# A PEER expert sweep walked by pairs of chunks instead of single chunks, with paired weight loads

## The chip, the core and the metric

The kernel is one program on one of the eight cores of a Trainium2 chip. The metric is device time in microseconds (us) of the whole program; lower is better. "PE" is the matrix engine, "DVE" the vector engine, "ACT" the scalar engine, "POOL" the engine that issues the gathers, "SP" the engine that issues the plain loads. All loads and gathers run on the same 16 DMA engines: what SP issues goes through queue q1 in the profile, what POOL issues through q0. Four runs of the kernel before were made: three for the time and one under the profiler.

## The reference

One decoder layer on 512 tokens of width 1024, in float32. First a mixer: eight heads of dilated window attention and eight of stick-breaking attention from one combined projection, an output projection, a residual and a LayerNorm. Then a PEER layer, cut here to what matters:

```python
q = (x @ w_query)                               # 8 heads, 2 halves of 128
scores = einsum(q, sub_keys)                    # 128 scores per half
top-16 per half -> 256 sums -> top-16 -> softmax gates, expert_idx in 0..16383
u = expert_u[expert_idx]                        # 128 experts per token
h = einsum('td,ted->te', x, u)
act = gates * gelu(h)
y = einsum('te,ted->td', act, expert_v[expert_idx])
x = LayerNorm(ALPHA * x + y)
```

The tables expert_u and expert_v have 16384 rows of 1024 floats, 64 MB each.

## The kernel before

The 512 tokens are four blocks of 128. The PEER layer is computed in two ways at once.

**Blocks 0 and 1, by gathers.** For each token and each of its 128 selected experts a row is fetched: one indirect DMA (`gather`, L790) fetches one selected row for each of 128 tokens, 512 KB in rows of 4 KB. There are 512 of them: 128 of U and 128 of V for block 0, then the same for block 1. The generator `gathers` (L826) issues them up to eight ahead of their use. A use (`gather_use`, L803) is one DVE instruction over 128 x 1024: a dot product for U (L808), a multiply-add into an accumulator for V (L819). A gather's buffer comes free with its use.

**Blocks 2 and 3, densely.** All 16384 experts are swept in 128 chunks of 128 experts, for the 256 tokens of both blocks. Chunk c has two parts:

- H(c), `h_part` (L918): eight products of a U chunk with the tokens, then a GELU on ACT (`gelu`, L910). The U chunk is loaded by `load_u` (L905) from a transposed copy of the table, 512 KB in rows of 4 KB, into one of WBUF = 4 buffers.
- Y(c), `y_mm` (L1229): the activation of the chunk, times its gates, times the V chunk, accumulated over all chunks. Most chunks are split into a high and a low part, three products each: `split_v` (L1177) rounds V on ACT (L1186) and subtracts on DVE (`low`, L126), `act_prep` (L1206) multiplies by the gates on DVE (L1210, L1211), rounds on ACT (L1221) and subtracts on DVE (L1227). The chunks that `plain` (L1174) names go through in one float32 product without a split. A split V buffer is free after the split; that of a plain chunk only after its Y.

The gates lie densely in memory: an earlier stage of 64 "gate steps" (one-hot products, `one_hot_b`, `gated`, `one_hot_2`, `g_mm`, `g_out`) writes them to a DRAM scratch `gd`, and the sweep reads them back in groups of eight chunks (`load_g`, L1026, called for chunk c+4 after chunk c; 960 KB in rows of 7.5 KB into one of two buffers `gt`).

**Order of the work.** The program runs in the order in which the Python code records it; each engine has one queue and goes through it strictly in order, so that an instruction that waits holds up all that stand behind it. The H parts of the first LEAD = 40 chunks are recorded early (`run_ahead`, L933), as filler of PE between other work; a burst of them runs in the routing of block 2 and some in each gate step. In the late gate steps, once the routing of blocks 3 and 1 is done, every fourth step also takes one gather (L1158). Then comes the main loop (L1303), for c from 0 to 121: `split_all(c)` prepares V up to chunk c+1 (more towards the end) and activations in pairs of chunks, then come as many gather uses as keep pace with a goal that reaches 512 at c = 116 (L1305; before c = 88 each chunk counts 1, after it 0.75), then H(c+40) while there is one, Y(c), the load of U chunk c+43, a group of gates, and V loads as far as buffers allow (`upto("l", ...)`, two pools of two buffers). H of the last chunk stands at c = 87; from c = 88 on pairs of chunks alternate between plain (88, 89, 92, 93, ... 120, 121) and split. The Y of the last KT = 6 chunks follow the loop (L1326 to L1332), first for block 2 over both halves, then for block 3, each with its LayerNorm (`final`, L1241) and output. The LayerNorms of blocks 0 and 1 are recorded into the loop, block 0 from c = 89 on, block 1 after the last gather.

Of the kernel before, what the change touches and what calls it, by code (L numbers as in the profile page):

```python
# [74 lines left out]
VBUF = 4  # L75
# [19 lines left out]
def build(ctx, nc, tc, a):  # L95
# [16 lines left out]
    wst = open_pool(ctx, "wst", "left", 2)  # L112
# [805 lines left out]
    def h_part(c, k0, k1):  # L918
        if k0 == 0:
            hps[c] = ps_h.tile([P, 512], F32, name="h", bufs=2)  # L920
        for k in range(k0, k1):
            nc.tensor.matmul(hps[c][:, :ND], us[c][:, k], xf[:, k], start=k == 0, stop=k == KD - 1)  # L922
# [10 lines left out]
    def run_ahead(n):  # L933
        out = None
        for _ in range(n):
            nxt_ = next(ahead, None)
            if nxt_ is None:
                break
            c, k = nxt_
            if k == 0:  # L940
                load_u(c + 3)
                if c and c - 1 in hps:
                    out = c - 1
            h_part(c, k, k + 1)
        if out is not None:
            gelu(out, hps.pop(out))
# [67 lines left out]
    r1 = open_pool(ctx, "r1", "right")  # L1014
# [17 lines left out]
    def load_v(c):  # L1032
        if c >= P:
            return
        vs[c] = vq[c // 2 % 2].tile([P, D], F32, name="v", bufs=2)
        nc.sync.dma_start(vs[c], a["peer_v"][c * P:(c + 1) * P])

    with tc.manual_schedule():
# [9 lines left out]
        for i in range(-1, NTASK + 2):  # L1048
# [30 lines left out]
            if i == 2 * NH:  # L1079
                for c in range(3):  # L1080
                    load_u(c)
# [5 lines left out]
        qs.close()  # L1087
        up = open_pool(ctx, "up", "left")
# [61 lines left out]
        for n in range(2):  # L1150
            load_v(n)
# [15 lines left out]
        rqs.close()  # L1167
        sgs.close()
        gtp.append(open_pool(ctx, "gt1", "left"))
        vq.append(open_pool(ctx, "vq1", "left"))  # L1170
        load_v(2)
# [18 lines left out]
        for c, k in ahead:  # L1190
            if k == 0:
                load_u(c + 3)
# [48 lines left out]
        def final(tb):  # L1241
# [7 lines left out]
            else:  # L1249
                y = wst.tile([P, D], F32, name="w", bufs=WBUF)  # L1250
# [20 lines left out]
        nxt = {"v": 1, "a": 2, "l": 3}  # L1271

        def upto(kind, last, use, at=P):
            now = []
            for c in range(nxt[kind], min(last, P - 1) + 1):
                if kind == "l" and plain(c - VBUF) and c - VBUF > at:
                    break
                now.append(c)
            nxt[kind] += len(now)
            for c in now:  # L1280
                use(c)
            return now

        def upto_a(last):
            now = []
            while nxt["a"] <= min(last, P - 1):
                c = nxt["a"]
                n = 2
                nxt["a"] += n
                act_prep(c, n, 1)  # L1290
                now.append((c, n))
            return now

        def split_all(c):
            ext = max(0, c - (P - 11))
            nv = upto("v", min(c + 5, c + 1 + (c > P - LEAD) + ext, nxt["l"] - 1), lambda k: split_v(k, 1))
            na = upto_a(c + 1 + max(0, ext - 1))
            for k in nv:
                split_v(k, 2)
            for k in na:  # L1300
                act_prep(*k, 2)

        for c in range(P - KT):  # L1303
            split_all(c)
# [7 lines left out]
            h_mm(c + LEAD)  # L1312
            for t in range(2):
                y_mm(t, c)
            load_u(c + LEAD + 3)
            load_g(c + 4)
            upto("l", nxt["v"] + 2, load_v, c)
            if c == P - LEAD:
                nc.scalar.preload_act_table_set("natural_log_exp_and_others")
                todo2 = final(0)  # L1320
                ln2 = []
                for n in ("ln2_g", "ln2_b"):
                    ln2.append(wst.tile([P, D], F32, name="w", bufs=WBUF))
                    nc.sync.dma_start(ln2[-1], a[n].to_broadcast([P, D]))
        upto("l", P, load_v)
        for c in range(P - KT, P):  # L1326
            split_all(c)
# [14 lines left out]
def layout(inputs):  # L1342
# [12 lines left out]
        "uT": f["peer_u"].reshape(P, P, KD, P).transpose(0, 3, 2, 1),  # L1355
# [19 lines left out]
```

## Time and profile before

| | us |
|---|---|
| median of three runs | 1468.81 (1466.58 to 1469.32) |
| time of the profiled execution | 1463.64 |
| its span, first to last instruction | 1461.9 |
| work ahead of the main loop's first Y | 0 to 744.8 |
| main loop with H and Y, c = 0 to 87 | 744.8 to 1288.3 |
| main loop with Y alone, to the last gather use | 1288.3 to 1414.6 |
| from there to the end | 1414.6 to 1461.9 |

The span is 1.7 us shorter than the execution's own time, and that execution is 5.2 us faster than the median of the three runs. PE is busy for 1375.1 us (94%), DVE 1176.7 (80%), POOL 672.0 (46%), ACT 479.1 (33%). A busy share is an average over stages with different limits; which one ends last is read stage by stage. A row of the timeline gives start, length, engine, line, operation, output<-inputs and, in brackets, the idle time ahead of it and what ended it.

### The profile page before, as it was taken

Reading aid. Unit: us, or ns where it says so; the run is one execution under the profiler, and the core shown is the slowest. Engines: PE = TensorE matmul, PEld = TensorE weight load, DVE = VectorE, ACT = ScalarE, POOL = GpSimd, SP = SyncE. Lnnn points to the kernel's source line nnn. Section 1 sums busy time; section 2 is a strip of 40 time slices with the busy share of each in tenths; the row PEclk is TensorE's granted clock in tenths of the full one; section 3 lists DMA queues with packets and bytes.
Section 4 is the critical chain, followed back from the end, with each engine's and each line's share of the span. In section 5 each row is a group of like instructions: output and inputs, shape, how many; then the busy total and the mean of one; then the engine's idle time right before and its main releaser. Section 6 shows DMA issues by size and latency. Waiting matters only on the chain.

```text
span 1461.9 us, 19349 instructions
## 1 busy us (share of the span) xinstructions
PE 1375.1 (94%) x6570; PEld 1101.9 (75%) x6570; DVE 1176.7 (80%) x2443; ACT 479.1 (33%) x962; POOL 672.0 (46%) x526
## 2 busy tenths in 40 slices
PE   8997999999989999799999999999999999987887
PEld 4676877766659998688988888888888888854444
DVE  1258998778789999899878877877777878798896
ACT  1322344264422111489932222222222222221121
POOL 0003577668554433100146566655555655656620
PEclk9999999999889999899999999999999999999999
DMA  8787899799889989767899999999999999999982
GB/s 297 252 268 280 299 368 321 276 377 343 303 290 376 329 286 317 240 182 207 245 349 410 409 410 409 409 410 410 409 409 410 409 409 410 409 405 411 410 312 94
DMA packets 162579, 495.92 MB, mean 339 GB/s; under 512 B 15376, under 2 KB 47520, under 8 KB 162480
## 3 DMA queue, kind: packets, MB, share of 16 engines
q0 software_dynamic: 74304, 270.12, 48.6%
q1 hardware_dynamic: 86448, 218.92, 41.2%
q10 hardware_dynamic: 1728, 5.64, 1.0%
q8 instruction: 52, 0.85, 0.2%
q14 instruction: 47, 0.39, 0.1%
HBM read 477.77 MB, written 16.84 MB: 338 GB/s over the span
## 4 chain that ended last, share of the span: by engine, by line
PE 49%; DMA 30%; DVE 13%; issue 4%; ACT 2%; POOL 1%; SPq 0%; DVEq 0%; POOLq 0%; ACTq 0%
DMA g<-peer_v,eidx 15%; PE h L922 14%; DMA g<-peer_u,eidx 12%; PE y L1238 7%; PE a L656 3%; PE b L656 3%; PE m L270 2%; PE m L553 2%; PE tr L553 1%; DVE g L808 1%; DMA v<-peer_v 1%; PE m L893 1%; PE h L347 1%; DVE o L875 1%; PE m L131 1%
## 5 line engine op out<-in xcount | busy, mean ns | idle before, releaser
L799 POOL DMA_INDIRECT g<-peer_u,eidx x256 | 349.9, 1367 | 325.7 <-DVE topi L600 123.5
L799 POOL DMA_INDIRECT g<-peer_v,eidx x256 | 316.2, 1235 | 396.9 <-DVE x L819 156.9
L922 PE MATMUL h<-xf,w 128*128 128x256 f32 x2048 | 472.0, 380 | 0.0
L922 PEld LDWEIGHTS h<-xf,w 128*128 128x128 f32 x2048 | 383.9, 191 | 51.8
L808 DVE SCALAR_TENSOR_TENSOR g<-g,x 128x1024 f32<-128x1024 f32 x256 | 305.5, 1220 | 45.9 <-DMA g<-peer_u,eidx 45.4
L1238 PE MATMUL y<-vh,a 128*128 128x512 f32 x816 | 255.5, 416 | 15.4 <-ACT a L1221 14.4
L1238 PEld LDWEIGHTS y<-vh,a 128*128 128x128 f32 x816 | 154.5, 191 | 54.8 <-ACT a L1221 21.4
L819 DVE SCALAR_TENSOR_TENSOR yg<-g,hg,yg 128x1024 f32<-128x1024 f32 x126 | 161.0, 1278 | 24.4 <-DMA g<-peer_v,eidx 24.1
L819 DVE SCALAR_TENSOR_TENSOR x<-g,hg,x 128x1024 f32<-128x1024 f32 x128 | 163.8, 1280 | 18.3 <-DMA g<-peer_v,eidx 18.2
L126 DVE TENSOR_TENSOR vl<-v,vh 128x1024 fp32r<-128x1024 f32 x105 | 128.1, 1221 | 48.9 <-ACT vh L1186 48.9
L914 ACT ACTIVATE gl<-h 128x256 f32<-128x256 f32 x128 | 48.7, 380 | 298.1 <-PE h L922 297.9
L1186 ACT ACTIVATE vh<-v 128x1024 fp32r<-128x1024 f32 x105 | 110.6, 1053 | 62.6 <-DMA v<-peer_v 62.5
L1238 PE MATMUL y<-vl,a 128*128 128x512 f32 x408 | 128.4, 396 | 0.7 <-DVE vl L126 0.7
L1221 ACT ACTIVATE a<-gl 128x512 fp32r<-128x512 f32 x51 | 32.0, 628 | 192.3 <-DVE gl L1211 192.3
L1238 PEld LDWEIGHTS y<-vl,a 128*128 128x128 f32 x408 | 77.2, 190 | 18.5 <-DVE vl L126 1.6
L1238 PE MATMUL y<-v,gl 128*128 128x512 f32 x144 | 65.6, 609 | 7.7 <-DVE gl L1210 7.7
L887 ACT ACTIVATE o<-o1b,sg 128x128 f32<-128x128 bf16 x216 | 70.6, 403 | 0.6 <-DVE o1b L869 0.5
L1238 PEld LDWEIGHTS y<-v,gl 128*128 128x128 f32 x144 | 27.4, 194 | 41.7 <-issue 30.1
L875 DVE TENSOR_TENSOR o<-sg,c_small 128x512 f32<-128x512 f32 x64 | 43.9, 686 | 9.3 <-PE m L893 4.4
L270 PE MATMUL m<-w,x0f 128*128 128x256 f32 (+1 forms) x128 | 45.8, 508 | 5.1 <-DMA w<-w_in 5.1
L130 PE MATMUL m<-wl,x2h 128*128 128x512 f32 x96 | 38.7, 403 | 7.9 <-DVE wl L126 7.9
L893 PEld LDWEIGHTS m<-o,o 128*128 128x128 f32 x304 | 39.4, 191 | 5.2 <-ACT gl L914 1.9
(301 smaller groups left out, 1871.4 us busy)
## 6 DMA issues: line engine op xcount, KB each, us to landing
w<-uT SPq DMA_DIRECT2D x128, 512.0 KB, 7.2
v<-peer_v SPq DMA_DIRECT2D x128, 512.0 KB, 8.9
w<-w_in SPq DMA_DIRECT2D x47, 512.0 KB, 4.9
gt<-gd SPq DMA_DIRECT2D x15, 960.0 KB, 11.1
w<-peer_wq SPq DMA_DIRECT2D x16, 512.0 KB, 4.4
wq<-peer_wq SPq DMA_DIRECT2D x16, 512.0 KB, 7.5
gd<-stage SPq DMA_DIRECT2D x15, 512.0 KB, 4.9
gd<-stage SPq DMA_DIRECT2D x15, 448.0 KB, 3.1
```

The lines of the kernel that those rows point to most:

```text
L126: nc.vector.tensor_sub(parts[1], src, parts[0].bitcast(F32))
L270: nc.tensor.matmul(ps[:, ch * wd:(ch + 1) * wd], x0f[:, kk], w[:, k], start=kk == 0, stop=kk == KD - 1)
L656: nc.tensor.matmul(qps[it][:, sl], w, x_, start=fresh and kk == n == 0, stop=kk == KD - 1, skip_group_check=True)
L799: nc.gpsimd.indirect_dma_start(out=u, out_offset=None, in_=a["peer_v" if kind else "peer_u"], in_offset=bass.IndirectOffsetOnAxis(ap=eidx[ ...
L808: nc.vector.scalar_tensor_tensor(u, u, 1.0, x, op0=OP.mult, op1=OP.mult, accum_out=hs[:, j:j + 1])
L819: nc.vector.scalar_tensor_tensor(acc, u, hs[:, j:j + 1], acc, op0=OP.mult, op1=OP.add)
L875: nc.vector.tensor_tensor(hot2[s], gate[tb][1][:, 0, t:t + TG, None].to_broadcast([P, TG, P]), iota[:, None, :].to_broadcast([P, TG, P]), ...
L887: nc.scalar.activation(hot[s][:, j], o1b[:, :, j], AF.Copy, scale=gate[tb][1][:, 1, t + j:t + j + 1])
L893: nc.tensor.matmul(gps[s][:, j * P:(j + 1) * P], o2[:, j], o1[:, j], start=True, stop=True)
L922: nc.tensor.matmul(hps[c][:, :ND], us[c][:, k], xf[:, k], start=k == 0, stop=k == KD - 1)
L1186: nc.scalar.activation(vsp[c][0], vs[c], AF.Copy)
L1238: nc.tensor.matmul(yps[t][hf], s_, w_[:, hf * 512:(hf + 1) * 512], start=c == 0 and n == 0, stop=c == P - 1 and n == len(terms) - 1)
```

## The change

1. **U in pairs.** The transposed copy `uT` is laid out by pairs of chunks, 1 MB each, in rows of 8 KB. `load_u(q)` loads pair q into one of two 1 MB buffers (before: four of 512 KB). It is called when the H of the second chunk of pair q-2 has been recorded.
2. **V in pairs.** A copy `v2` of the V table, also in rows of 8 KB; `load_v(q)` loads a pair into one of three 1 MB buffers (VBUF = 3; before: four buffers of 512 KB). A pair's buffer is loaded again once both its chunks are split, or, if plain, once their Y are recorded (`upto_v`).
3. **The loop by pairs.** For c = 0, 2, 4, ...: V is split up to c+2 (a plain pair: up to c+3), activations are prepared up to c+3, then half of the gathers, H(c+40), H(c+41), the other half, Y(c), Y(c+1), V loads, a group of gates.
4. **Plain chunks** end two earlier: 120 and 121 are now split. The preparation for the last chunks is spread differently.
5. **Late gate steps** take a gather in every second step instead of every fourth. The count of gathers used when the main loop begins goes from 219 to 224 of 512.
6. The output tiles of blocks 2 and 3 and the two LayerNorm rows live in the pair tiles of U; some memory pools are opened and closed at other places.

The diff, cut to its core:

```diff
-VBUF = 4
+VBUF = 3
...
-    def load_u(c):
-        if c < P:
-            us[c] = wst.tile([P, KD, P], F32, name="w", bufs=WBUF)
-            nc.sync.dma_start(us[c], a["uT"][c])
+    def load_u(q):
+        if q < P // 2:
+            t = wst.tile([P, 2, KD, P], F32, name="w", bufs=2)
+            nc.sync.dma_start(t, a["uT"][q])
+            for i in range(2):
+                us[2 * q + i] = t[:, i]
...
         if k1 == KD:
             del us[c]
+            if c % 2:
+                load_u(c // 2 + 2)
...
-        vs[c] = vq[c // 2 % 2].tile([P, D], F32, name="v", bufs=2)
-        nc.sync.dma_start(vs[c], a["peer_v"][c * P:(c + 1) * P])
+    def load_v(q):
+        t = vq[q % VBUF].tile([P, 2, D], F32, name="v")
+        nc.sync.dma_start(t, a["v2"][q])
+        for i in range(2):
+            vs[2 * q + i] = t[:, i]
...
                 limit = NG
-                if s % 4 == 0:
+                if s % 2 == 0:
                     run(head(gs, 1))
...
         def plain(c):
-            return P - LEAD <= c < P - KT and c // 2 % EVERY == 0
+            return P - LEAD <= c < P - KT - 2 and c // 2 % EVERY == 0
...
+        def upto_v():
+            while nxt["l"] < P // 2 and all(k in used for k in (2 * (nxt["l"] - VBUF), 2 * (nxt["l"] - VBUF) + 1)):
+                load_v(nxt["l"])
+                nxt["l"] += 1
...
-        for c in range(P - KT):
-            split_all(c)
...
-            h_mm(c + LEAD)
-            for t in range(2):
-                y_mm(t, c)
-            load_u(c + LEAD + 3)
-            load_g(c + 4)
-            upto("l", nxt["v"] + 2, load_v, c)
+        for c in range(0, P - KT, 2):
+            end = max(0, c - (P - KT - 6)) // 2
+            split_all(c + 2 + plain(c) + (0, 1, 4)[end], c + 2 + (0, 2, 4)[end])
+            gather_to(c)
+            for k in range(2):
+                h_mm(c + LEAD + k)
+            gather_to(c + 1)
+            for k in range(2):
+                for t in range(2):
+                    y_mm(t, c + k)
+            used.update((c, c + 1))
+            upto_v()
+            for k in range(2):
+                load_g(c + k + 4)
...
-        "uT": f["peer_u"].reshape(P, P, KD, P).transpose(0, 3, 2, 1),
+        "v2": f["peer_v"].reshape(P // 2, 2, P, D).transpose(0, 2, 1, 3),
+        "uT": f["peer_u"].reshape(P // 2, 2, P, KD, P).transpose(0, 4, 1, 3, 2),
```

How the order moves, at two places. First SP in the part of the loop without H, from the V loads behind chunk 92 on; before, `v` are single chunks and `gt` is the group of gates for chunks 96 to 103; a name in brackets is the engine or DMA lane waited for, PE standing for the Y of a plain chunk and DVE for a split.

```order
L1036 DMA v_9750<-peer_v 128x1024 [waits DMAHW5_49,DMAHW1_49,PE_49]
L1324 DMA w_9753<-ln2_g 128x1024
L1324 DMA w_9755<-ln2_b 128x1024 [waits DMAHW3_49]
L1036 DMA v_9783<-peer_v 128x1024 [waits DMAHW6_49,DMAHW4_49,PE_49]
L1036 DMA v_9785<-peer_v 128x1024 [waits DMAHW7_49,DVE_49]
L1036 DMA v_9815<-peer_v 128x1024 [waits DMAHW0_49,DVE_49]
L1030 DMA gt_9857<-gd_111 128x1920
```

And in the changed kernel at the same place; `v` are pairs, `gt_9668` the group for chunks 96 to 103.

```order
L1038 DMA v_9566<-v2 128x2048 [waits DMAHW7_49,PE_49]
L1038 DMA v_9568<-v2 128x2048 [waits DMAHW1_49,DVE_49]
L1338 DMA w_9571<-ln2_g 128x1024 [waits DMAHW6_49]
L1338 DMA w_9571<-ln2_b 128x1024
L1038 DMA v_9664<-v2 128x2048 [waits DMAHW3_49,DMAHW0_49,PE_49]
L1038 DMA v_9666<-v2 128x2048 [waits DMAHW4_49,DVE_49]
L1034 DMA gt_9668<-gd_111 128x1920
```

The group of gates now stands right behind two V pairs, and these wait for the Y of the plain pair 92, 93.

Second DVE before the first gate product of that group (`gl` with `gt_9857`, chunks 96 and 97), before; `vl` with `v` is the split of a chunk, `x2` and `yg` with `g` are gather uses.

```order
L1210 TENSOR_TENSOR gl_8366<-gl_8366,gt_9621 128x2x240
L1211 TENSOR_TENSOR gl_8366<-gl_8366,glast_4222 128x2x16
L126 TENSOR_TENSOR vl_9862<-v_9815,vh_9861 128x1024
L1227 TENSOR_TENSOR a_9866<-gl_8366,a_9866 128x2x256
L819 SCALAR_TENSOR_TENSOR x2_100<-g2_9773,hg1_108,x2_100 128x1024
L819 SCALAR_TENSOR_TENSOR yg_2349<-g2_9787,hg1_108,yg_2349 128x1024
L819 SCALAR_TENSOR_TENSOR x2_100<-g2_9790,hg1_108,x2_100 128x1024
L819 SCALAR_TENSOR_TENSOR yg_2349<-g2_9819,hg1_108,yg_2349 128x1024
L1210 TENSOR_TENSOR gl_8447<-gl_8447,gt_9857 128x2x240
L1211 TENSOR_TENSOR gl_8447<-gl_8447,glast_4222 128x2x16
L819 SCALAR_TENSOR_TENSOR x2_100<-g_9822,hg1_108,x2_100 128x1024
```

And in the changed kernel at the first gate product with `gt_9668`; the rows with `mv` and `lw` belong to the LayerNorm of block 0.

```order
L820 SCALAR_TENSOR_TENSOR yg_2349<-g2_9555,hg1_108,yg_2349 128x1024
L820 SCALAR_TENSOR_TENSOR x2_100<-g2_9576,hg1_108,x2_100 128x1024
L1265 SCALAR_TENSOR_TENSOR x2_100<-x2_100,mv_9591,w_9571 128x512
L1266 SCALAR_TENSOR_TENSOR x2_100<-x2_100,lw_9593,w_9571 128x512
L1215 TENSOR_TENSOR gl_8316<-gl_8316,gt_9668 128x2x240
L1216 TENSOR_TENSOR gl_8316<-gl_8316,glast_4218 128x2x16
L820 SCALAR_TENSOR_TENSOR yg_2349<-g2_9579,hg1_108,yg_2349 128x1024
L820 SCALAR_TENSOR_TENSOR x2_100<-g_9585,hg1_108,x2_100 128x1024
L820 SCALAR_TENSOR_TENSOR yg_2349<-g_9588,hg1_108,yg_2349 128x1024
L820 SCALAR_TENSOR_TENSOR x2_100<-g_9638,hg1_108,x2_100 128x1024
```

In both, the gate product heads a round of DVE, and the gather uses stand behind it. Before, the load of the group is recorded after chunk 92 and this product in the preparation at chunk 95. Now the load is recorded at the end of the round of chunks 92 and 93 and the product at the start of the next round, that of chunks 94 and 95. In the same way every later group (104, 112, 120) follows two V pairs and stands one round ahead of its product.

More of the change, by code (lines that the diff above doesn't have):

```diff
@@ L111, in build @@
     g3 = open_pool(rqs, "g3", "right")
-    wst = open_pool(ctx, "wst", "left", 2)
+    wss = ExitStack()
+    wst = open_pool(wss, "wst", "left", 2)
     qs = ExitStack()
@@ L939, in run_ahead @@
             c, k = nxt_
[L940 to L943, printed above, removed]
+            if k == 0 and c and c - 1 in hps:
+                out = c - 1
             h_part(c, k, k + 1)
@@ L1013, in build @@
     yg.append(g2[0].tile([P, D], F32, name="yg"))
-    r1 = open_pool(ctx, "r1", "right")
+    r1s = ExitStack()
+    r1 = open_pool(r1s, "r1", "right")
     rp = open_pool(rqs, "rp", "right")
@@ L1078, in build @@
                 fill = chain(fill, project_out(fill_at), normalize(fill_at))
-            if i == 2 * NH:
-                for c in range(3):
-                    load_u(c)
         for g_ in after:
@@ L1087, in build @@
         qs.close()
+        wss.close()
+        wst = open_pool(ctx, "uw", "left")
+        for q in range(2):
+            load_u(q)
         up = open_pool(ctx, "up", "left")
@@ L1149, in build @@
         third, late = route_steps(3), route_steps(1)
-        for n in range(2):
-            load_v(n)
+        load_v(0)
         for s in range(NS):
@@ L1167, in build @@
         rqs.close()
+        r1s.close()
         sgs.close()
@@ L1170, in build @@
         vq.append(open_pool(ctx, "vq1", "left"))
+        vq.append(open_pool(ctx, "vq2", "left"))
+        load_v(1)
         load_v(2)
@@ L1249, in final @@
             else:
-                y = wst.tile([P, D], F32, name="w", bufs=WBUF)
+                if not ylast:
+                    ylast.append(wst.tile([P, 2, D], F32, name="w", bufs=2))
+                y = ylast[0][:, tb - 2]
                 for hf, sl in enumerate(sls):
@@ L1271, in build, with upto, split_all, gather_to @@
         nxt = {"v": 1, "a": 2, "l": 3}
[L1273 to L1278, printed above, removed]
+        ylast, used = [], set()
+        def upto(kind, last):
+            now = list(range(nxt[kind], min(last, P - 1) + 1))
             nxt[kind] += len(now)
-            for c in now:
-                use(c)
-            return now
[L1284 to L1297, printed above, removed]
+            return now
+        def upto_v():
+            while nxt["l"] < P // 2 and all(k in used for k in (2 * (nxt["l"] - VBUF), 2 * (nxt["l"] - VBUF) + 1)):
+                load_v(nxt["l"])
+                nxt["l"] += 1
+        def split_all(last_v, last_a):
+            nv = upto("v", min(last_v, 2 * nxt["l"] - 1))
+            for k in nv:
+                split_v(k, 1)
+            na = []
+            while nxt["a"] <= min(last_a, P - 1):
+                na.append(nxt["a"])
+                nxt["a"] += 2
+                act_prep(na[-1], 2, 1)
             for k in nv:
                 split_v(k, 2)
+            used.update(k for k in nv if not plain(k))
             for k in na:
-                act_prep(*k, 2)
-        for c in range(P - KT):
-            split_all(c)
+                act_prep(k, 2, 2)
+            upto_v()
+        def gather_to(c):
+            nonlocal todo2
             goal = min(NG, pre - (-(NG - pre) * spent(0, c) // spent(0, GEND)))
@@ L1311, in build @@
             next(todo2, None)
-            h_mm(c + LEAD)
-            for t in range(2):
-                y_mm(t, c)
-            load_u(c + LEAD + 3)
-            load_g(c + 4)
-            upto("l", nxt["v"] + 2, load_v, c)
+        used.add(0)
+        for c in range(0, P - KT, 2):
[9 more added lines that the diff above has]
+            used.update((c, c + 1))
+            upto_v()
+            for k in range(2):
+                load_g(c + k + 4)
             if c == P - LEAD:
@@ L1320, in build @@
                 todo2 = final(0)
[L1321 to L1325, printed above, removed]
+                lnt = wst.tile([P, 2, D], F32, name="w", bufs=2)
+                ln2 = [lnt[:, i] for i in range(2)]
+                for t, n in zip(ln2, ("ln2_g", "ln2_b")):
+                    nc.sync.dma_start(t, a[n].to_broadcast([P, D]))
         for c in range(P - KT, P):
-            split_all(c)
+            split_all(c + 4, c + 4)
         run(todo2)
```

5 lines of the change are left out of this document (removed).

## Prediction

> **What bounds the kernel now.** I read the stages first, by windows: PE, weight load, DVE, ACT and POOL busy time, then the granted PE clock, the DMA share and GB/s. The stages are the work ahead of the sweep, the loop with H and Y, the loop with Y alone until the last gathers, and the end.
>
> ```profile
> 0.00:744.78 744.78, 695.90 (x3715) 560.62 (x3715) 594.28 (x1677) 307.00 (x702) 281.02 (x238) 0.97 0.85 294
> 744.78:1288.27 543.49, 542.36 (x2449) 461.98 (x2449) 438.85 (x583) 141.28 (x221) 319.60 (x231) 1.00 1.02 407
> 1288.27:1412.05 123.78, 101.72 (x292) 57.16 (x292) 107.73 (x121) 19.85 (x24) 70.26 (x56) 0.94 1.02 406
> 1412.05:1461.90 49.85, 35.11 (x118) 22.16 (x116) 35.82 (x65) 10.95 (x17) 1.16 (x2) 0.92 0.35 118
> ```
>
> In the second stage PE never rests and DMA is full too (share 1.02): two bounds at once. In the third PE rests 22 us, DVE 16, and DMA alone stays full. The chain of waits gives PE's pace in the second stage, and the timeline its first plain pair behind it:
>
> ```profile
> 753.98 3.45 PE h L922 x16
> 757.44 2.73 PE y L1238 x12
> ...
> 1288.27 7.03 PE L1238 MATMUL y<-v,gl 128*128 128x512 f32 x16
> ```
>
> A chunk costs 3.45 + 2.73 = 6.18 us. The stage holds 87 H (the first stands ahead of it) and 88 Y: 87 x 3.45 + 88 x 2.73 = 540.4 us of its 543.5. What DMA must carry meanwhile is 1.05 MB of U and V, 0.12 of gates and 293/109 = 2.69 gathers of 0.524 MB per chunk (a goal of 293 over 109 weighted chunks): 2.58 MB in 6.18 us, 417 GB/s. Full DMA moves less, and what it moves changes while a group of gates is in flight. The first and third row are the 12.4 us behind the issue of such a group, the others the rest of its period:
>
> ```profile
> 864.02:876.40 12.38, 12.38 (x57) 10.58 (x56) 9.45 (x16) 3.18 (x5) 6.98 (x5) 1.00 1.02 412
> 876.40:912.50 36.10, 36.10 (x165) 30.89 (x164) 29.47 (x46) 8.57 (x15) 21.56 (x15) 1.00 1.03 409
> 963.01:975.39 12.38, 12.38 (x57) 10.58 (x56) 9.54 (x16) 3.18 (x5) 8.26 (x6) 1.00 1.03 411
> 975.39:1011.50 36.11, 36.11 (x165) 30.91 (x164) 28.85 (x45) 8.94 (x15) 19.24 (x16) 1.00 1.03 409
> ```
>
> So the stage lacks 417 - 409 = 8 GB/s, 4.4 MB over 543 us, which the eight gathers in flight (4.2 MB) just cover; the third stage inherits the debt.
>
> **Rows of 8 KB.** Gates are the one load with rows near 8 KB (7.5). During their transfer, 819.5 to 822.5, and in a stretch without them, 826.9 to 833.1, the two queues (packets, MB, share of the engines) read:
>
> ```profile
> q1 hardware_dynamic: 114, 0.80, 65.1%
> q0 software_dynamic: 116, 0.41, 35.7%
> ...
> q0 software_dynamic: 356, 1.29, 52.4%
> q1 hardware_dynamic: 347, 1.25, 50.3%
> ```
>
> Packets alternate one for one in both, and a packet is a row. Two things follow for U and V. First the rate: 411.5 against 409 with 0.98 of 5.1 MB (19%) in long rows makes them 0.6/0.19 = 3% faster; U and V are 41% of the loop's bytes, so 409 becomes about 414 (bounds 409 and 417). Second, SP's loads get two thirds of the engines against gathers, 0.80 MB in 3 us = 267 GB/s, where it was half.
>
> The Trainium skill (DMA: Bandwidth & Descriptors, section SWDGE vs HWDGE vs iDMA) has packets of preferably at most 4096 B as the unit at which an engine switches between queues. By that an 8 KB row would go in two turns, with neither gain nor larger share; the rows above speak against it for the plain loads, where a 7.5 KB row is one packet. What it would do is the slower rival below.
>
> **Ahead of the loop: 0 us** (-1 to +4). The burst of H in the routing of block 2 now has the next U pair issued when the pair before the current one is done, with 6.9 us (two H) to land. From the chain, then DMA of that stretch, then landing times of the single U loads (least, median, most):
>
> ```profile
> 543.66 39.73 PE h L922 x184
> ...
> 543.66:583.41 39.75, 39.75 (x185) 34.99 (x185) 39.58 (x165) 4.70 (x12) 12.56 (x13) 1.00 0.91 314
> ...
> DMA to landing us min/median/max: 3.3/7.2/12.6
> ```
>
> The least, 3.3 us for 0.524 MB, is 1.3 us at 409 GB/s and 2.0 fixed. A pair (1.05 MB) then takes 2.0 + 2.6 = 4.6 us alone and 2.0 + 3.9 = 5.9 at two thirds: below 6.9, so PE goes on; +4 is six boundaries each 0.7 late. The five more gathers cost DVE about 1.2 us each, in gate steps where PE is the bound and DVE has 2.4 of 10 us idle:
>
> ```profile
> 710.00:720.00 10.00, 10.00 (x70) 9.41 (x69) 7.63 (x13) 9.46 (x28) 1.48 (x1) 1.00 0.89 290
> ```
>
> Four steps take 7.5 us there, so the extra use fits in the 1.8 idle.
>
> **Loop with H: -2.5 us** (-3 to +2). The need falls to 288/109 = 2.64 gathers, 2.55 MB and 413 GB/s, about what DMA gives at 414; the debt is gone, and of the 543.5 - 540.4 = 3.1 us that PE lost I take back 2.5. H, H, Y, Y is the same PE work. A group of gates now lands later against its product, but DVE's work per pair, from the rows below, is 0.67 + 2 x 1.14 + 0.60 + 5.28 x 1.20 = 9.9 of 12.4 us, and the 2.5 idle absorb it over four pairs.
>
> ```profile
> 1294.47 0.65 DVE L1210 TENSOR_TENSOR gl<-gl,gt 128x480 f32<-128x480 f32 x1
> 1295.04 0.19 DVE L1211 TENSOR_TENSOR gl<-gl,glast 128x32 f32<-128x32 f32 x1
> 1295.14 2.35 DVE L126 TENSOR_TENSOR vl<-v,vh 128x1024 fp32r<-128x1024 f32 x2
> 1297.41 0.68 DVE L1227 TENSOR_TENSOR a<-gl,a 128x512 fp32r<-128x512 f32 x1
> 1298.01 1.28 DVE L819 SCALAR_TENSOR_TENSOR x<-g,hg,x 128x1024 f32<-128x1024 f32 x1
> 1299.21 1.28 DVE L819 SCALAR_TENSOR_TENSOR yg<-g,hg,yg 128x1024 f32<-128x1024 f32 x1
> ```
>
> (From start to start: gate products 0.67, a split 1.14, the second part 0.60, a use 1.20.)
>
> **Loop with Y alone: -2.5 us** (-8 to +12). By bytes it should shrink more. Before it ran 126.3 us, from 1288.3 to the end of the last use at 1414.6. But now the group of gates stands on SP right behind two V pairs that wait for a plain Y, and its product heads DVE's next round. Before, it had slack; issue and first use of the group of chunk 96:
>
> ```profile
> 1297.89 0.43 SPq L1030 DMA_DIRECT2D gt<-gd  x1
> ...
> 1322.75 0.65 DVE L1210 TENSOR_TENSOR gl<-gl,gt 128x480 f32<-128x480 f32 x1
> ...
> 1413.35 1.28 DVE L819 SCALAR_TENSOR_TENSOR yg<-g,hg,yg 128x1024 f32<-128x1024 f32 x1
> ```
>
> That is 25 us, and DVE did not wait. Now the group lands, after the plain Y ends, 2.0 + 3.08 MB (two pairs and the gates): at 267 GB/s 13.5 us, at 409 with no gather in the way 9.5. I take 12.5, since freed gather buffers keep q0 going during most of it. With chunk 88's Y at 0: PE ends Y(92, 93) at 7.0 + 5.5 + 7.0 = 19.5, so the gates land at 32, where DVE, with its 29 us of work, would be ready at 29.4. From there a plain round costs DVE 0.67 + 2.28 + 0.60 + 4.78 = 8.3, a split round 0.67 + 4.78 = 5.45. The next plain pair that releases a group, four rounds on, has its product three rounds and one product later, at 5.45 + 8.33 + 0.67 = 14.5, its Y ends at 21.5 and its gates land at 34; DVE alone would be back at 27.6, DMA alone (16 gathers, 8 V, one group, 13.6 MB at 414) at 32.8. So a period of eight chunks takes 34, with DVE waiting 6 us in each. Two periods, then 24.0 of DVE (5.45 + 8.33 + 5.45 + 4.75) to the last use: 32 + 68 + 24 = 124. The low bound is 9.5 us and DMA's 32.8: 29.4 + 65.6 + 24 = 119; the high one is the slower rival's.
>
> **The end: -3 us** (-6 to +2). Here the last V loads waited for the plain Y of 120 and 121:
>
> ```profile
> 1418.58 14.29 PE y L1238 x40
> 1432.87 0.02 issue
> 1432.88 0.33 SPq L1036
> ...
> 1433.79 5.49 DMA v<-peer_v
> ...
> 1442.36 1.91 PE y L1238 x7
> ```
>
> Those chunks are split now, a pair costing PE 5.5 instead of 7.0, and the pairs behind them come with chunk 117's Y. DVE then sets the end: from the last use 8.0 us until the group of chunk 120 has landed (its Y ends 2.5 ahead of that use, then 10.5 with few gathers left), 17.1 of products, splits and block 1's LayerNorm to the last split, 1.7 until PE is through block 2, 36 x 0.228 = 8.2 for block 3 (2.73/12 = 0.228 a product), and 9.1 behind PE's end as before: 44.1 instead of 1461.9 - 1414.6 = 47.3.
>
> **The rivals.**
>
> *Faster.* If the gathers have landed when a group of gates is called, SP has the engines to itself, the group lands in 9.5 us, and DMA is the bound: -2.5, 119 for 126.3 (-7.3), the end one us better (-4): -14, 1455. For it: DMA in the third stage is full now. Against it: four uses fall in each wait and refill q0. Chance 0.2.
>
> *No change.* The long rows bring nothing over many loads, DMA stays at 409 against a need of 413, DVE enters the third stage 5 us late, and PE's 2.5 stay lost: -8 + 5 + 2.5, about -0.5. For it: 411.5 over 409 is a small reading. Chance 0.2.
>
> *Slower.* The change does not give what its rows promise: 8 KB rows are cut in two, SP keeps half (204 GB/s), and the group behind two pairs lands after 2.0 + 15.1 = 17 us. Then 36.5 + 2 x 38.5 + 24 = 137.5 for the third stage, +11; the end -1, the loop with H -1: +9, 1478. It decides from a landing of about 14.5 us on, where three waits of 2 us and the end's have eaten the 8. For it: the rule above, and that the gates now have no slack. Against it: 114 packets of 0.80 MB. Chance 0.18.
>
> **The numbers.** The forecast is the sum 0 - 2.5 - 2.5 - 3 = -8 us, made on the profiled execution: span 1454, its own time 1463.6 - 8 = 1455.6. The three runs' median lies 5.2 above it, and I take the difference over to that: 1468.8 - 8 = 1461. Its chance is 0.42. A measurement here tells about 0.2%, 3 us, from no change. Faster is forecast and first rival, 0.62; same 0.2; slower 0.18. The range reaches from 1450, a little beyond the faster rival, to 1472, which leaves out most of the slower one.
>
> **What would show it.** DVE's gate product waits for its load 3 to 6 us at chunks 96, 104, 112 and 120, with V loads just ahead on SP; q1 moves rows of 8 KB as single packets, two thirds of the bytes while both queues are full; GB/s in the loop about 414; the third stage still near 124. Wrong would be no wait at the gates (faster rival), DMA at 409 (no change), or PE gaps ahead of H by late U pairs.

## The result and the profile after

The changed kernel is slower: 1480.2 us median (1479.3 to 1482.2, four runs) against 1467.7 (1464.9 to 1469.3, four runs), a ratio of 1.0089 with a 95% interval of 1.0069 to 1.011. The two profiled executions lie a little further apart, 1478.2 against 1461.9 us of span. The windows of the changed kernel, cut at the same events as those of before (first Y, first plain Y, end of the last gather use):

```profile
0.00:752.56 752.56, 698.96 (x3730) 562.49 (x3731) 603.87 (x1687) 310.13 (x705) 289.77 (x243) 0.97 0.84 296
752.56:1296.52 543.96, 539.75 (x2435) 460.66 (x2434) 428.63 (x579) 148.43 (x219) 310.26 (x230) 1.00 1.01 404
1296.52:1432.84 136.32, 102.95 (x306) 59.59 (x305) 105.24 (x121) 19.12 (x24) 60.00 (x52) 0.87 0.91 351
1432.84:1478.20 45.36, 30.53 (x113) 22.86 (x111) 33.54 (x61) 11.24 (x18) 1.17 (x2) 0.81 0.31 121
```

The first Y now has two H of the loop ahead of it instead of one, so 3.45 us must go over from the first row to the second before the kernels are compared. Then the front is 4.3 us longer, the loop with H 3.9 longer, the stage of Y alone 10.0 longer (136.3 against 126.4), the end 1.9 shorter: 16.3 in all. In the third row DMA is not full any more (0.91, was 1.02) and PE's clock is down from 0.94 to 0.87, so both wait for something else. Two groups of the page name it; behind the second bar stands the idle time ahead of a group, and what ended it:

```profile
L1215 DVE TENSOR_TENSOR gl<-gl,gt 128x480 f32<-128x480 f32 x64 | 41.9, 654 | 105.4 <-DMA gt<-gd 105.4
L1243 PE MATMUL y<-v,gl 128*128 128x512 f32 x128 | 63.3, 652 | 33.4 <-DVE gl L1215 33.4
```

DVE waits 105.4 us for groups of gates (before: none), and PE 33.4 us for the products of DVE behind them. The timeline of DVE shows where: the first row is the place in the loop with H where PE stopped longest, the other four are chunks 96, 104, 112 and 120, each with its idle time in brackets:

```profile
1191.62 0.66 DVE L1215 TENSOR_TENSOR gl<-gl,gt 128x480 f32<-128x480 f32 x1 [9.10 <-DMA gt<-gd]
...
1331.54 0.66 DVE L1215 TENSOR_TENSOR gl<-gl,gt 128x480 f32<-128x480 f32 x1 [6.49 <-DMA gt<-gd]
...
1370.57 0.66 DVE L1215 TENSOR_TENSOR gl<-gl,gt 128x480 f32<-128x480 f32 x1 [11.34 <-DMA gt<-gd]
...
1408.77 0.66 DVE L1215 TENSOR_TENSOR gl<-gl,gt 128x480 f32<-128x480 f32 x1 [10.50 <-DMA gt<-gd]
...
1440.43 0.66 DVE L1215 TENSOR_TENSOR gl<-gl,gt 128x480 f32<-128x480 f32 x1 [3.34 <-DMA gt<-gd]
```

These are the places that the prediction named; it had given them 3 to 6 us. SP's rows for the second of the four show two V pairs held until 1354.6, when PE is done with a plain pair, and the gates behind them:

```profile
1354.58 0.80 SPq L1038 DMA_DIRECT2D v<-v  x2
1355.44 0.42 SPq L1034 DMA_DIRECT2D gt<-gd  x1
```

And what the queues moved from there, in stretches of 2 us (packets, MB, share of the engines): 1355.4 to 1357.4, 1357.4 to 1359.4, 1367.4 to 1369.4 and 1369.4 to 1371.4:

```profile
q0 software_dynamic: 227, 0.82, 102.2%
...
q0 software_dynamic: 140, 0.50, 63.2%
q1 hardware_dynamic: 42, 0.34, 41.5%
...
q1 hardware_dynamic: 70, 0.48, 57.3%
q0 software_dynamic: 90, 0.34, 42.9%
...
q0 software_dynamic: 215, 0.79, 98.5%
q1 hardware_dynamic: 12, 0.03, 3.9%
```

The gathers (q0) fill the engines while the loads have not begun, for 3.5 us from the first issue, and keep going to the end. Between the ends, from 1359.4 to 1367.4, the queues stand as forecast: as many packets in both, two thirds of the engines for SP's loads.

```profile
q1 hardware_dynamic: 308, 2.23, 67.2%
q0 software_dynamic: 306, 1.11, 34.5%
```

So the gates, asked for when PE ends at 1354.6, are there at 1370.6: 16.0 us, where I had taken 12.5.

### The profile page after: what moved, and what is told of

Read it like the earlier page. It is cut to its first block, busy times and chain, and to the rows that moved or that the text cites. A ratio compares the mean times of both kernels' runs of the same rounds, so it can differ in the third digit from the quotient of the medians.

```text
span 1478.2 us, 19012 instructions
## 1 busy us (share of the span) xinstructions
PE 1372.2 (93%) x6578; PEld 1105.6 (75%) x6578; DVE 1171.3 (79%) x2446; ACT 488.9 (33%) x965; POOL 661.2 (45%) x526
## 4 chain that ended last, share of the span: by engine, by line
PE 53%; DMA 22%; DVE 12%; issue 8%; POOL 2%; ACT 1%; SPq 0%; POOLq 0%; DVEq 0%; ACTq 0%
PE h L925 14%; PE y L1243 12%; DMA g<-peer_u,eidx 10%; DMA gt<-gd 6%; PE a L657 3%; PE b L657 3%; PE m L271 2%; POOL g L800 2%; DMA g<-peer_v,eidx 2%; DVE g L809 2%; DMA w<-uT 2%; PE m L554 1%; PE tr L554 1%; PE m L894 1%; PE h L348 1%
## 5 line engine op out<-in xcount | busy, mean ns | idle before, releaser
L800 POOL DMA_INDIRECT g<-peer_u,eidx x256 | 358.4, 1400 | 319.9 <-DVE topi L601 123.4
L800 POOL DMA_INDIRECT g<-peer_v,eidx x256 | 296.8, 1160 | 426.7 <-DVE x L820 194.1
L925 PE MATMUL h<-xf,w 128*128 128x256 f32 x2048 | 466.3, 381 | 3.6 <-DMA w<-uT 3.6
L809 DVE SCALAR_TENSOR_TENSOR g<-g,x 128x1024 f32<-128x1024 f32 x256 | 302.6, 1223 | 40.3 <-DMA g<-peer_u,eidx 39.8
L1243 PE MATMUL y<-vh,a 128*128 128x512 f32 x816 | 238.9, 404 | 0.0
L820 DVE SCALAR_TENSOR_TENSOR x<-g,hg,x 128x1024 f32<-128x1024 f32 x128 | 167.5, 1309 | 7.3 <-DMA g<-peer_v,eidx 7.2
L820 DVE SCALAR_TENSOR_TENSOR yg<-g,hg,yg 128x1024 f32<-128x1024 f32 x126 | 164.7, 1307 | 3.7 <-DMA g<-peer_v,eidx 3.5
L1215 DVE TENSOR_TENSOR gl<-gl,gt 128x480 f32<-128x480 f32 x64 | 41.9, 654 | 105.4 <-DMA gt<-gd 105.4
L917 ACT ACTIVATE gl<-h 128x256 f32<-128x256 f32 x128 | 47.3, 380 | 160.1 <-PE h L925 160.0
L1243 PE MATMUL y<-v,gl 128*128 128x512 f32 x128 | 63.3, 652 | 33.4 <-DVE gl L1215 33.4
## 6 DMA issues: line engine op xcount, KB each, us to landing
gt<-gd SPq DMA_DIRECT2D x15, 960.0 KB, 12.6
```

What stands on the lines that cost most here:

```text
L800: nc.gpsimd.indirect_dma_start(out=u, out_offset=None, in_=a["peer_v" if kind else "peer_u"], in_offset=bass.IndirectOffsetOnAxis(ap=eidx[ ...
L809: nc.vector.scalar_tensor_tensor(u, u, 1.0, x, op0=OP.mult, op1=OP.mult, accum_out=hs[:, j:j + 1])
L820: nc.vector.scalar_tensor_tensor(acc, u, hs[:, j:j + 1], acc, op0=OP.mult, op1=OP.add)
L917: nc.scalar.activation(gls[c // 2][:, c % 2], ps[:, :ND], AF.Gelu)
L1243: nc.tensor.matmul(yps[t][hf], s_, w_[:, hf * 512:(hf + 1) * 512], start=c == 0 and n == 0, stop=c == P - 1 and n == len(terms) - 1)
```

## The experiments

The theory (A) is that late gates cost the time. The main rival (B) is that DMA's bytes are the bound, and the waits for gates only stand where other waits would be. Times are medians of the experiment; ratios are to the kernel before, run beside them on the same chip (before: 1468.2 us beside the first four, 1466.4 beside the next four, 1469.1 beside the last four). The table splits one profiled execution of each: to the last routing product ahead of the burst of H; from there to the loop's first H (the first Y less one H of 3.45, or two); the loop with H from there to the first plain Y; Y alone to the last gather use; the end.

| | median, us | ratio (95%) | to burst | to loop | loop with H | Y alone | end |
|---|---|---|---|---|---|---|---|
| before | 1467.7 | | 542.8 | 198.5 | 546.9 | 126.4 | 47.3 |
| changed | 1480.2 | 1.0089 (1.0069 to 1.011) | 543.5 | 202.1 | 550.9 | 136.3 | 45.4 |
| 1 gates ahead of V | 1463.8 | 0.9961 (0.9932 to 0.999) | 548.1 | 200.6 | 551.3 | 124.0 | 42.0 |
| 2 and a round earlier | 1457.6 | 0.993 (0.9908 to 0.9952) | 541.6 | 203.2 | 544.0 | 124.5 | 42.0 |
| 3 changed, U single | 1481.4 | 1.0079 (1.0048 to 1.011) | 545.6 | 198.7 | 552.4 | 137.7 | 45.3 |
| 4 changed, 4 KB rows | 1506.8 | 1.0235 (1.0188 to 1.0282) | 548.1 | 205.5 | 568.3 | 147.3 | 47.2 |
| 5 = 2, 4 KB rows | 1458.5 | 0.9956 (0.9936 to 0.9975) | 541.8 | 199.0 | 544.0 | 126.5 | 41.9 |
| 6 = 2, U single | 1456.5 | 0.9928 (0.9903 to 0.9952) | 549.3 | 198.7 | 544.0 | 125.2 | 41.9 |
| 7 = 2, every 4th step | 1462.4 | 0.9963 (0.9943 to 0.9983) | 550.6 | 205.1 | 544.1 | 128.5 | 41.9 |
| 8 = 2, 120 and 121 plain | 1454.9 | 0.9922 (0.9892 to 0.9952) | 543.5 | 203.7 | 544.0 | 124.7 | 39.8 |
| 9 = 2 with 6 and 8 | 1456.0 | 0.991 (0.9892 to 0.9928) | 546.3 | 198.9 | 544.0 | 125.1 | 43.3 |
| 10 before, late gates | 1472.2 | 1.0034 (1.0019 to 1.0048) | 537.8 | 199.9 | 546.6 | 131.8 | 47.4 |
| 11 before, every 2nd step | 1460.6 | 0.9947 (0.993 to 0.9964) | 539.4 | 199.8 | 544.5 | 122.3 | 46.0 |
| 12 = 9, every step | 1467.2 | 0.9978 (0.9957 to 0.9998) | 546.4 | 213.8 | 544.1 | 122.4 | 39.5 |

The column "to burst" says how to read the rest: several of these programs are the same up to there (1, 2, 7 and 8, for instance), and single executions still spread from 541.6 to 550.6. A few us of the total are the front's chance; the later columns are steadier, though the next one still spreads from 200.6 to 203.7 over the changed kernel and experiments 1, 2 and 8, which are one program up to the loop. The profiled execution need not be near the median: in 4 and 7 it is the slowest of its experiment (1518.3 and 1472.0), in 11 the fastest (1453.8).

**1. Gates ahead of the V pairs of their round.**

```diff
-            upto_v()
             for k in range(2):
                 load_g(c + k + 4)
+            upto_v()
```

> The changed kernel, but in each round the group of gates is recorded ahead of the V pairs of that round instead of behind them; this moves it only in the part of the loop without H (chunks 96, 104, 112, 120). Theory A (the gates' place behind V pairs that wait for a plain Y makes DVE, and with it PE, wait): the three waits of 6.5, 11.3 and 10.5 us ahead of the gate product and the 3.3 of the last group go, the stage of Y alone falls from 136.3 us (chunk 88's Y to the last gather use) to 120 to 125, the total by 10 to 14, to about 1467; the 70 us of waits for gates in the loop with H stay. Rival B (DMA's bytes are the bound, and the waits for gates only stand where others would be): DVE waits for gathers or V instead, the total stays within 4 us of 1480.

Measured: 1463.8, Y alone 124.0, the loop with H 551.3 as it was. DVE's waits for gates in the stage of Y alone and at the end are gone; 80.7 us of them stay, all ahead of that stage:

```profile
L1215 DVE TENSOR_TENSOR gl<-gl,gt 128x480 f32<-128x480 f32 x64 | 41.8, 653 | 80.7 <-DMA gt<-gd 80.7
```

This is theory A, with a little more than it asked; B falls.

**2. And a round earlier.**

```diff
-                load_g(c + k + 4)
+                load_g(c + k + 6)
```

> As the first, and the group of gates a whole round (two chunks) earlier as well, in the loop with H too. Theory A: every wait of a gate product for its load goes, also those of 3 to 11 us in the loop with H; PE's idle there (3.6 + 0.6 us, and its low clock behind the 3.6) goes too, so the loop with H, 550.8 us from its first H to chunk 88's Y, falls to 545 to 547, and the total is 4 to 6 below the first experiment, about 1462. Rival B (the waits in the loop with H are absorbed, as forecast, and PE's loss there has another cause): the loop with H stays at 549 to 551, the total at that of the first experiment.

Measured: 1457.6. No gate product waits for its load any more, and the loop with H is at 544.0, PE's own time (88 x 6.18 = 543.8). In the view of the gates (`--tile gt`) the list of waits is empty, while the loads take about as long to land, 11.8 us in the median and up to 18.4 (changed kernel: 12.6 and 15.9):

```profile
its engine sat idle before it (us, times) until:
who waited for it (us, times):
...
DMA to landing us min/median/max: 11.1/11.8/18.4
```

So what was missing is the time between a load and its use, not a faster load. The rival of this experiment falls too: the waits in the loop with H were not absorbed. By the two, late gates cost 1480.2 - 1457.6 = 22.6 us (23 by the ratios), and the changed kernel without them beats the kernel before by 0.7%.

**3. U in single chunks.**

```diff
-            t = wst.tile([P, 2, KD, P], F32, name="w", bufs=2)
-            nc.sync.dma_start(t, a["uT"][q])
+            us[c] = wst.tile([P, KD, P], F32, name="w", bufs=4)
+            nc.sync.dma_start(us[c], a["uT"][c // 2][:, c % 2])
```

> The changed kernel with U loaded in single chunks again (rows of 4 KB out of the paired layout, four buffers of 512 KB, each loaded again as soon as its own chunk's H is done); V stays in pairs. Theory A (two pair buffers give the burst of H too little lead): the gaps of PE for U in the burst, 3.0 us more than before, and the 1.1 at the loop's first H go, the front ends about 4 us earlier; the loop with H, where gates stand behind one short U load less, changes by -3 to +2; total 1474 to 1478. Rival B (the burst's gaps come from what the queues carry, not from the buffers' lead): the gaps stay within 1 us of those of the changed kernel, total 1480 or more.

Measured: 1481.4, a miss by 3.4 us in the total. The part that A speaks of came: from the burst to the loop 198.7 instead of 202.1, no gap in the burst. The first fence is the chain of waits in the burst of the changed kernel, the second in this one:

```profile
544.37 5.20 PE h L925 x24
549.58 8.57 DMA w<-uT
558.29 14.07 PE h L925 x64
572.37 7.39 DMA w<-uT
579.90 10.61 PE h L925 x48
```

```profile
546.40 39.73 PE h L923 x184
586.15 3.87 DMA w<-uT
```

The two pairs of U that PE waited for took 8.6 and 7.4 us to land (the other five of the burst 4.9 to 7.7), and the two buffers give them 6.9. How far the cause goes is not shown, for this run changes the length of the rows and the size of a load along with the lead. Experiment 5, with the same two pair buffers but two loads of 4 KB rows to each, has no gap in the burst either (front 199.0), experiment 4, the same program up to the loop, has one of 0.9 us, and experiment 1, with loads as in the changed kernel, has 0.1 in all there. What the front gains, the loop with H and Y alone lose (1.5 and 1.4), and this execution came to the burst 2.0 later. Experiments 6 and 9 show the same in the front, 198.7 and 198.9.

**4. The changed kernel with 4 KB rows.**

```diff
-            nc.sync.dma_start(t, a["uT"][q])
+            for i in range(2):
+                nc.sync.dma_start(t[:, i], a["uT"][q][:, i])
```

(and the same for V)

> The changed kernel with every pair of U and V loaded by two DMAs of 4 KB rows, issued together into the same buffers at the same places. Theory A (rows of 8 KB are faster by about 1.2 % while DMA is full, and give SP's loads two thirds against the gathers): DMA falls from 414 to 409 GB/s where it is full, SP's queue gets half of it instead of two thirds, the groups of gates in the stage without H land in 16 to 18 us instead of 15, and the total rises by 3 to 9, to 1483 to 1489. Rival B (only bytes count): the rate, the landings and the total stay within 2 us.

Measured: 1506.8, 27 us more: A in its direction, SP's share and landings, three to nine times its price. Where both queues are full, 1388 to 1400, each has half:

```profile
q1 hardware_dynamic: 638, 2.59, 53.6%
q0 software_dynamic: 647, 2.36, 49.5%
```

The gates of that stage land 16.6 to 17.8 us after their issue, and DVE waits longer at each, 138.6 us in all:

```profile
1402.79 0.66 DVE L1217 TENSOR_TENSOR gl<-gl,gt 128x480 f32<-128x480 f32 x1 [13.78 <-DMA gt<-gd]
...
1445.21 0.66 DVE L1217 TENSOR_TENSOR gl<-gl,gt 128x480 f32<-128x480 f32 x1 [14.74 <-DMA gt<-gd]
```

In the loop with H, where the changed kernel's PE stood still twice, this one's stops at nearly every group, and the loop takes 568.3 us (in the profiled execution, which is 11.5 us above the median).

**5. Early gates with 4 KB rows.** (2 and 4 together.)

> The second experiment (gates a round earlier, ahead of V) with every pair of U and V loaded by two DMAs of 4 KB rows. Theory A (rows of 8 KB are worth their rate, 414 against 409 GB/s, also where no gate waits): the need of 413 GB/s in the loop with H is not met, that loop takes 546 to 549 us instead of 544, the stage of Y alone inherits the debt and grows by 3 to 8, the total is 1463 to 1470. Rival B (the 4 KB rows of the fourth experiment cost their 27 us only through the late gates, and with early gates row length does not matter): 1456 to 1460.

Measured: 1458.5, rival B. The rate did fall as A said. Windows of 400 us in the middle of the loop, first with 8 KB rows (experiment 2), then with 4 KB (experiment 5); the last figures are DMA's share and GB/s:

```profile
800.00:1200.00 400.00, 400.00 (x1814) 342.58 (x1813) 321.09 (x465) 109.82 (x163) 243.64 (x173) 1.00 1.02 413
```

```profile
800.00:1200.00 400.00, 400.00 (x1814) 342.39 (x1813) 316.86 (x460) 112.06 (x163) 234.85 (x169) 1.00 1.03 409
```

But PE is busy for all 400 us in both: 4 GB/s less leave the loop at 544.0, and only 2.0 us appear in the stage of Y alone. So row length cost 27 us where gates were late and 1 where they were early, by the medians; by the ratios it is 4, with intervals that overlap.

**6. Early gates with single U.** (2 and 3 together.)

> The second experiment with U in single chunks (four buffers, 4 KB rows), V in pairs. Theory A (the two pair buffers of U cost the front about 4 us, and with V alone in long rows DMA still gives about 411.5 GB/s, a little under the need of 413): front -4, loop with H 544 to 546, the stage of Y alone at most 3 longer, total 1453 to 1457. Rival B (the rate is worth more than the front): loop with H 547 or more, total 1458 to 1463.

Measured: 1456.5, by A's stages: the front 198.7, the loop 544.0, Y alone 0.7 longer. Against experiment 2 the total is within the uncertainty.

**7. Early gates, a gather in every fourth late gate step.**

```diff
-                if s % 2 == 0:
+                if s % 4 == 0:
```

> The second experiment with a gather in every fourth late gate step again, so that 219 instead of 224 gathers are used when the loop begins. Theory A (DMA's bytes count): five gathers more, 2.6 MB, cost 6.3 us at 414 GB/s, of which the loop with H hides some; total 1460 to 1464. Rival B (they are hidden, as the loop with H now stands at PE's 544 us): total 1456 to 1459, with a front that is the same or up to 2 shorter.

Measured: 1462.4, theory A: the five gathers cost 4.8 us against experiment 2, 4.0 of them in Y alone; the two intervals just overlap.

**8. Early gates, chunks 120 and 121 plain.**

```diff
-            return P - LEAD <= c < P - KT - 2 and c // 2 % EVERY == 0
+            return P - LEAD <= c < P - KT and c // 2 % EVERY == 0
```

> The second experiment with chunks 120 and 121 plain again, as in the kernel before. Theory A (the end's gain, 47.3 us before and 42.0 in the second experiment, comes from splitting these two chunks): the end grows to 44 to 47, the total to 1460 to 1463. Rival B (the end's gain comes from V being there earlier, and a plain pair spares DVE 3.5 us at the end): 1455 to 1458.

Measured: 1454.9, just below B's range; end 39.8. The gain at the end comes without splitting the two chunks, so A falls. In this execution the split costs 2 us; experiment 9 doesn't repeat that.

**9. Early gates, single U and plain 120 and 121.** (2, 3 and 8 together.)

> The second, sixth and eighth experiment together: gates a round earlier and ahead of V, U in single chunks, chunks 120 and 121 plain. Theory A (the three gains lie in different stages and add up: 4.4 us in the front, 2.1 at the end): burst of H to the loop 198.7, loop with H 544, Y alone 124 to 126, end 40; total 1451 to 1454. Rival B (the plain pair at the end and U's shorter rows both load the stage of Y alone and take it back there): 1455 to 1458.

Measured: 1456.0, which is B's number. The front's gain came (198.9), the end's did not (43.3, where experiment 6 with the two chunks split has 41.9). Experiments 2, 6, 8 and 9 all beat both kernels; which of them is best, these runs don't tell.

**10. Late gates in the kernel before.**

```diff
-            load_g(c + 4)
+            load_g(c + 2)
```

> The kernel before, with one number changed: each group of gates is loaded two chunks later, so that its load stands one chunk ahead of its product, as close as in the changed kernel; chunks, rows and buffers are as before. Theory A (late gates alone make a kernel slower, pairs or not): DVE waits 3 to 8 us at the gate product of most groups, the total rises by 4 to 12, to 1471 to 1479. Rival B (it takes the pairs, with 2 MB of V in one wait ahead of the gates): waits under 2 us, total within 2 us of before.

Measured: 1472.2, slower by 0.3% (0.2 to 0.5), A at its lower end. DVE waits 39.2 us in ten places, at three of them in Y alone:

```profile
1323.37 0.66 DVE L1210 TENSOR_TENSOR gl<-gl,gt 128x480 f32<-128x480 f32 x1 [4.25 <-DMA gt<-gd]
...
1359.81 0.66 DVE L1210 TENSOR_TENSOR gl<-gl,gt 128x480 f32<-128x480 f32 x1 [5.08 <-DMA gt<-gd]
...
1395.64 0.66 DVE L1210 TENSOR_TENSOR gl<-gl,gt 128x480 f32<-128x480 f32 x1 [3.30 <-DMA gt<-gd]
```

Y alone is 5.4 us longer. Late gates cost without pairs too. In the changed kernel the waits at the same three places are one and a half to three times as long; that 2 MB of V ahead of the gates make the difference fits experiment 1, where these waits go, but no run tries it alone.

**11. More late gathers in the kernel before.** (The edit of 7 the other way, from 4 to 2.)

> The kernel before, with only the late gate steps changed: a gather in every second instead of every fourth. Theory A (five gathers fewer in the loop are worth the 4.8 us that the seventh experiment lost without them): 1460 to 1464. Rival B (in the kernel before, the loop's loss has another cause, and the gathers are hidden or cost the gate steps as much): 1465 to 1469.

Measured: 1460.6, A: 0.5% faster than before, 2.4 us of it in the loop with H and 4.1 in Y alone. This one number of the change is worth about as much as all of it with its gates mended (1457.6, with overlapping intervals). What the rest of the change brings, about 3 us by these two, can't be told from nothing.

**12. A gather in every late gate step.**

```diff
-                if s % 2 == 0:
-                    run(head(gs, 1))
+                run(head(gs, 1))
```

> The ninth experiment with a gather in every late gate step, some ten more ahead of the loop. Theory A (each gather taken there spares DMA 1.27 us and DVE 1.20 in the stage of Y alone, as the step from the seventh to the second experiment showed): 5 to 9 us below the ninth. Rival B (DVE, 36 of 44 us busy in the late gate steps, becomes their bound with 12 us more, and PE waits there): the front grows by 4 or more, the total is within 3 us of the ninth.

Measured: 1467.2, 11 us above experiment 9, worse than either theory. The late gate steps are B's: the front grows by 14.9 us, DVE (third figure with a bracket behind it) is busy for 49.5 of 50 us from 690 on, and PE waits 7.0 us for U at the loop's first H:

```profile
690.00:740.00 50.00, 45.99 (x279) 39.02 (x279) 49.53 (x86) 39.55 (x112) 25.28 (x16) 0.97 0.87 293
```

```profile
757.18 10.18 PE L923 MATMUL h<-xf,w 128*128 128x256 f32 x32 [6.96 <-DMA w<-uT]
```

Y alone and the end are shorter by 2.7 and 3.7 only.

## Why the prediction was wrong, step by step

The sum was -8 us; on the profiled executions it came to +16.3, 24.3 off. Half of that, 12.5, is one term, the loop with Y alone: the landing of the gates behind two V pairs, 12.5 us in the sum, took 16.0, and PE came back from the wait at half its clock, which the sum did not have. 6.4 more is the loop with H, whose waits for gates the sum held to be absorbed, and 4.3 the front.

**What bounds the kernel, and the rows.** DMA full and PE full in the loop held, and so did the debt: with five gathers fewer in the kernel before, the loop with H goes from 546.9 to 544.5 (experiment 11). Rows of 8 KB gave what was forecast, 413 to 414 GB/s for 409 and two thirds of the engines. By the rule of the Trainium skill that I had weighed (DMA: Bandwidth & Descriptors, section SWDGE vs HWDGE vs iDMA), units of 4096 B would have given SP half; the trace disagrees, 308 packets of 2.23 MB against 306 of 1.11. What I had wrong is what it is worth: 1 to 4 us once the gates are early (experiment 5), where the no-change rival put the lost rate at 7.5.

**The front, 0 forecast, +4.3 measured.** 0.7 is the spread ahead of the burst. The other 3.6 are PE's waits for U, two in the burst and one of 1.14 us at the loop's first H; the page's group of H has their sum behind the second bar:

```profile
L925 PE MATMUL h<-xf,w 128*128 128x256 f32 x2048 | 466.3, 381 | 3.6 <-DMA w<-uT 3.6
```

The step that failed is the landing of a U pair, 5.9 us forecast from a transfer at two thirds of the engines; six of the seven in the burst took 6.3 to 8.6. It stands against 6.9, so the margin of one us was none. The waits are inside the range that the term had (+4), and their size is that of one execution (experiment 3).

**The loop with H, -2.5 forecast, +3.9 measured.** The step that failed: "the 2.5 idle absorb it over four pairs". SP's queue holds the gates behind a V pair that waits for a split on DVE, and behind a U pair. They land up to 15.9 us after their issue, and DVE waits 1 to 11 us. Most of that was absorbed: PE stood still for DVE twice only, for 0.6 and 3.6 us. The chain shows the second place:

```profile
1175.66 15.94 DMA gt<-gd
...
1192.38 1.15 DVE vl L127
1193.53 0.04 issue
1193.58 3.77 PE y L1243 x10
1197.35 7.33 PE h L925 x32
```

PE waits 3.6 us, and the pieces behind are long (a pair of H takes 6.91 elsewhere). From the H at 870.6 to the one at 1222.5 there are 28 rounds of 12.36 us, 346.1, and it took 351.9: 5.9 us lost, 5.6 of them in the two rounds at this place. Waits of DVE as long or longer, 10.9 us at 791.8 and at 1242.6, cost PE 0.6 us and nothing; this group took longest to land of those in the loop with H; why PE stopped here and not there was not followed further. An average of idle time over four pairs says nothing about one wait of 9 us.

**Y alone, -2.5 forecast, +10.0 measured.** The mechanism was right in place and kind, and the size wrong: the first of these groups came 3 us later than in the sum, and the two periods of eight chunks behind it took 39.0 and 38.2 us instead of 34. I had taken 12.5 us from the plain Y's end to the gates, between 9.5 and the slower rival's 17, because freed gather buffers would keep q0 going only part of the time. It went on all the time. The 3.08 MB at two thirds and 2.0 us fixed make 13.5, 1.0 more than I took; the other 2.5 went to the start and the end. From the first issue to the first packet 3.5 us passed, from the last data to the landing 0.6, and q1 thins out over the last two; for all this I had 2.0, from the shortest landing of a load of U. Measured, 16.0: past the 14.5 from which the prediction let the slower rival decide. The second size was PE's. I had let the next plain Y end 21.5 us after the gates; it ended after 23.0, though DVE's product was there after 14.5 as forecast, for this reason: behind the wait PE ran at half its clock.

```profile
1332.25 9.98 PE L1243 MATMUL y<-v,gl 128*128 128x512 f32 x16 [10.93 <-DVE gl L1215]
```

```profile
1332.00:1335.40 3.40, 3.15 (x4) 1.51 (x5) 3.40 (x5) 0.00 (x0) 1.64 (x1) 0.50 1.02 412
1335.40:1338.80 3.40, 3.40 (x6) 1.36 (x5) 3.40 (x5) 0.63 (x1) 2.48 (x4) 0.61 0.80 271
1338.80:1342.20 3.40, 3.40 (x9) 1.49 (x9) 3.40 (x5) 0.00 (x0) 1.01 (x2) 1.00 0.92 292
```

A plain pair of 7.03 us takes 9.98 after 10.9 us of idling: a granted clock of 0.50, then 0.61, then 1.00, which is half the clock for 5.8 us and full from there; after the next two waits it is 4.3 and 3.6. The Trainium skill (TensorE: Matmul & The Clock Gate, section What's actually happening) has this rule: after an idle window of about 3.4 us the array runs at half its clock until a window of work has passed. The rows agree for these waits; but in the kernel before the clock was 0.50 from 1334.0 to 1337.4 too, behind a wait of only 2.5 us that ended at 1333.1. The half clock was missing from my sum, which let PE come back at full speed, though the row of that stage before already had 0.94. With both, a period of eight chunks is 1370.6 - 1331.5 = 39.0 us, where I had 34.

**The end, -3 forecast, -1.9 measured,** with a wait of 3.3 us for the last group of gates in it. With early gates it is -5.3 (experiment 2). The reason I gave, that the split chunks 120 and 121 cost PE less, is not borne out: with both plain and early gates the end is 39.8, 43.3 and 39.5 (experiments 8, 9 and 12), with both split 41.9 to 42.0. The other edit at the end, the preparation of the last chunks, was not tried alone.

**The rivals.** The slower one came nearest in time, +9 and 1478, with a wrong cause: rows were not cut and SP had its two thirds. That a wrong cause gave the right time is luck; the right one, the gates' missing slack, was in the forecast with a price that was 3.5 us per group too low. The faster rival failed at its condition, that the gathers have landed when the gates are called, and the one of no change at its own, that DMA stays at 409 GB/s.

**What paid and what cost.** Late gathers about -6 (4.8 by experiments 2 and 7, 8.5 by experiment 11 against before), late gates about +23, and the rest of the change the difference to the measured +12.5, about -4, uncertain by as much.

## What to carry to other kernels

A load that waits for nothing must not stand on its queue behind loads that wait for a buffer: it lands with them, however early it could have gone. When a change makes transfers larger, recount for every load behind them the time from its issue to its first use, with the queue ahead of it and full engines in the way, and compare that with the slack at each use, not with the idle time of an average round. And try the small edits of a bundle alone: here one number was worth about as much as the whole change with its gates mended.

## What the runs showed of the hardware

- Rows of 8 KB and of 4 KB go as single packets, and the two queues alternate one for one; so SP's loads had 67% of the engines with 8 KB rows against gathers of 4 KB (308 packets of 2.23 MB to 306 of 1.11), and about half with 4 KB rows (638 of 2.59 MB to 647 of 2.36). Full DMA moved 413 GB/s against 409.
- With the engines full of gathers, at the one place looked at, a load's first packet came 3.5 us after its issue, and the landing of the last load 0.6 us behind its last data.
- After 10.9 us of idling PE had half its clock for 5.8 us: 3 us lost on a plain pair, on top of the wait. In the kernel before a wait of 2.5 us was enough for 3.4 us of half clock.
- The same program came to the burst of H at 541.6 to 550.6 us in single executions; what makes this spread was not looked into.
